# Another order of the projection pairs in a hybrid decoder block, and another place for the first SSD step

## The chip, the core and the metric

The kernel runs on one core of a Trainium2 chip. The metric is the device time of one execution in microseconds (us). Five engines work side by side, each through its own queue in order: TensorE (PE in the profile, its weight loads PEld), VectorE (DVE), ScalarE (ACT), GpSimd (POOL) and SyncE (SP). Loads and stores are DMAs, issued here from the queues of SP and ACT.

## The reference

One decoder layer over 1024 positions with a width of 1024, all in float32:

```
u    = rmsnorm(x)
proj = u @ w_in        # gate_a | gate_s | B_a | C_a | v_a | z | xBC | dt
y_a  = (B_a * causal_conv3(C_a * v_a)) @ w_a_out
xbc  = silu(causal_conv4(xBC) + b)                  # 16 tiles of x, 4 of B, 4 of C
y    = ssd_scan(x, softplus(dt), B, C) + d_skip * x # 32 heads, 4 groups, chunks of 128
y_s  = group_rmsnorm(y * silu(z)) @ w_s_out
h    = x + (sigmoid(gate_a) * y_a + sigmoid(gate_s) * y_s) @ w_o
v    = rmsnorm(h)
out  = rmsnorm(h + (silu(causal_conv3(v @ w_1) + b) * (v @ w_3)) @ w_down)
```

The SSD scan works on chunks of 128 positions, one group of 8 heads after the other: within a chunk a masked product of C, B and x, and between chunks a state of 128 x 512 that decays.

## The kernel before

**Products.** Precision comes from splitting each float32 operand in a high part (written by ACT, line 148) and a low part (the difference, on POOL or DVE, line 149), and adding three matmuls per pair of operands. A product of a 128-column weight block is 12 matmuls (line 259). The projection is made in *pairs* of two 128-channel blocks over all 1024 positions by a Strassen-Winograd scheme with 7 products instead of 8, so a pair is 84 matmuls. The seven results go through PSUM and are combined on DVE (lines 287 to 318) to the two output rows of 128 x 1024. The seven left operands (U) are made once and fill all 14 big buffers until the last pair has used them.

**Kinds of pairs.** 37 pairs are run by the two lists of the change, by kind and first block:
- `xb` (xBC): two s4 tiles for the inputs of the convolution; then for each channel block a convolution of one ACT and three DVE instructions over 128 x 1024 (lines 535 and 539), Silu (line 546) and a store to the DRAM buffer ssd_in (line 548). xb 0 to 14 are x of groups 0 to 3 (four blocks a group), xb 16 and 18 are B of groups 0, 1 and 2, 3; xb 20 and 22 are C of the same.
- `z`: two b4 tiles, Silu, store to ssd_in (lines 563 and 564).
- `ca`, `ba`: C_a, v_a and B_a of the short convolution; ca uses one s4 and one b4 tile, ba two s4 tiles. Four DVE instructions and a product; the result is stored.
- `gs`, `ga`: gates, two b4 tiles, Tanh and a store.

There are three s4 and three b4 tiles, so a pair's tiles are waited for if earlier ones are still in the convolution or in a store.

**The SSD beside the pairs.** `BEFORE` is run first. Then each product of a pair in `BESIDE` advances a clock by one tick, and the parts of the SSD's steps are called at fixed ticks: step s (group s // 8, chunk s % 8) has its base at D0 + DSTEP * s, and its eight parts at the offsets of STAGES: the loads m (line 633) and in (line 636, six blocks of ssd_in: four of x, one of B, one of C) at -9; the decay matrix on ACT at -6; transposes px, pb and the product pc (lines 648 to 652) with their consumers at -4; loads for z and the decay at -3; the matmuls pd, po and pst (lines 690 to 703) with DVE's adds and the state on POOL at 0; squares at 3; the norm's sum pn at 6, and after each fourth chunk a transpose pr. A step's loads and its store go through ACT's queue.

**Order.** These calls give each instruction a priority in program order. A planner that simulates the engines then fixes each queue's order: a later instruction goes ahead when its inputs and its buffers are free in the simulation. At run time each engine works through its queue in order.

**After the pairs** come y_a (64 products over half the positions at a time, two halves), s_out, out_proj and the feed-forward part. w_sums, eleven calls beside s_out and y_a, prepares sums and differences of w_down for the last products: two loads of 512 KB into s4 tiles (tile wd, line 793), four subtractions on DVE and POOL (line 784), four stores (line 801).

Of the kernel before, what the change touches and what calls it, by code (L numbers as in the profile page):

```python
# [39 lines left out]


BEFORE = (
    ("xb", 16), ("z", 0), ("xb", 18), ("z", 2), ("xb", 20), ("xb", 22), ("xb", 0), ("xb", 2),
)
BESIDE = (
# [4 lines left out]
)  # L50


D0, DSTEP = 11, 6
STAGES = LOAD_M, LOAD_IN, DECAY, TRANS, LOAD_Z, DIAG, SQUARES, NORM = -9, -9, -6, -4, -3, 0, 3, 6


# [1181 lines left out]
```

## Time and profile before

| what | value |
|---|---|
| median of 3 runs | 2004.32 us (2004.31 to 2005.55) |
| profiled execution | 2004.03 us, span 2002.3 us |
| granted TensorE clock, mean | 0.986 |
| PE busy | 96% of the span |
| DVE, POOL, ACT busy | 72%, 65%, 46% |

Lines of the timeline give start, length, engine, source line and operation with output <- inputs; where the engine stood idle just ahead, its idle time and what ended it follow in brackets. Sums over stretches give for each stretch the busy time of the engines and the number of their instructions, then the granted clock of TensorE, the DMA engines' busy share and what they moved. A table of waits names who waited, for whom, the total, the number of times and the longest. A tile's table gives minimum, median and maximum in ns, and the first and last start. Matmuls overlap in the pipeline, so their busy times can sum to more than a stretch.

The pairs of the two lists run from about 110 to 996 us; the SSD's matmuls from 289 to 996 us.

### The profile page before, as it was taken

How to read it: one execution, taken by the hardware profiler on the slowest of the kernel's cores; microseconds unless marked ns; L12 is line 12 of the kernel's file. 1: busy time of each engine (PE TensorE's matmuls, PEld its weight loads, DVE VectorE, ACT ScalarE, POOL GpSimd, SP SyncE). 2: the span in 40 equal slices, each digit the busy share in tenths (PEclk: the TensorE clock that was granted, in tenths of full speed). 3: DMA queues.
4: the chain of work that ended last, by engine and by line, in shares of the span. 5: the costliest groups of instructions: out<-in, count | busy, mean ns of one | idle time of the engine just before them, and what ended most of it. 6: DMA issues, size and time to landing. Idle time of an engine off the chain costs nothing.

```text
span 2002.3 us, 26005 instructions
## 1 busy us (share of the span) xinstructions
PE 1923.3 (96%) x8986; PEld 1575.2 (79%) x8986; DVE 1450.9 (72%) x1616; ACT 918.0 (46%) x1697; POOL 1292.9 (65%) x931
## 2 busy tenths in 40 slices
PE   6899989999999999998999999988999999999998
PEld 5778877788788778776788888877888888887886
DVE  8956886787888778786884724379877788884445
ACT  5354445556655855444443323354433333343434
POOL 7667776776767677677545423368887888853542
PEclk9999999999999999999999999998999999999999
DMA  4244234444534554387897645442322244477654
GB/s 153 51 141 143 95 121 153 148 152 144 190 119 151 167 168 144 113 267 254 317 409 251 225 151 188 159 165 81 130 85 102 104 153 153 153 242 261 217 184 157
DMA packets 180179, 338.46 MB, mean 169 GB/s; under 512 B 15280, under 2 KB 87760, under 8 KB 179024
## 3 DMA queue, kind: packets, MB, share of 16 engines
q1 hardware_dynamic: 93264, 253.95, 37.1%
q10 hardware_dynamic: 86784, 82.85, 13.0%
q8 instruction: 71, 1.16, 0.2%
q14 instruction: 60, 0.49, 0.1%
HBM read 247.34 MB, written 89.41 MB: 168 GB/s over the span
## 4 chain that ended last, share of the span: by engine, by line
PE 64%; DVE 14%; DMA 7%; issue 5%; POOL 4%; ACT 4%; ACTq 0%; SPq 0%; POOLq 0%; DVEq 0%
PE so L259 9%; PE ya L259 4%; DVE cv L539 4%; PE pt2up L259 3%; PE pt3up L259 3%; PE pb22up L259 3%; PE pt4up L259 3%; PE pb11up L259 3%; PE pt1up L259 3%; PE pb21up L259 3%; PE d L1031 2%; PE d L1032 2%; PE d L1033 2%; DMA wd<-in_w_down 1%; PE wo L904 1%
## 5 line engine op out<-in xcount | busy, mean ns | idle before, releaser
L539 DVE SCALAR_TENSOR_TENSOR cv<-xbc,scw,cv 128x1024 f32<-128x1024 f32 x72 | 128.8, 1800 | 20.8 <-ACT cv L535 20.5
L642 ACT ACTIVATE m<-m,tk 128x128 f32<-128x128 f32 x256 | 79.1, 391 | 101.0 <-DMA m<-acd 88.5
L539 DVE SCALAR_TENSOR_TENSOR fcv<-fci,fcw,fcv 128x1024 f32<-128x1024 f32 x44 | 85.9, 1953 | 28.5 <-ACT fcv L535 28.5
L149 POOL TENSOR_TENSOR l_ws<-raw_ws,h_ws 128x512 fp32r<-128x512 f32 x32 | 46.4, 1450 | 74.6 <-PE so L259 43.1
L148 ACT CAST h_ws<-raw_ws 128x512 fp32r<-128x512 f32 x64 | 39.4, 622 | 99.1 <-PE so L259 67.5
L259 PE MATMUL so<-yh,h_ws 128*128 128x512 f32 x256 | 68.8, 391 | 0.0
L259 PE MATMUL so<-yl,h_ws 128*128 128x512 f32 x256 | 68.6, 389 | 0.0
L259 PE MATMUL so<-yh,l_ws 128*128 128x512 f32 x256 | 68.5, 389 | 0.0
L149 POOL TENSOR_TENSOR l_wo<-raw_wo,h_wo 128x512 fp32r<-128x512 f32 x24 | 31.6, 1316 | 53.9 <-PE wo L905 36.5
L149 DVE TENSOR_TENSOR l_wo<-raw_wo,h_wo 128x512 fp32r<-128x512 f32 x24 | 25.2, 1050 | 51.7 <-ACT h_wo L148 26.9
L661 ACT ACTIVATE xe<-px,tk 128x64 f32<-128x64 f32 x256 | 55.5, 326 | 13.2 <-DVE xd L654 13.2
L148 ACT CAST h_wo<-raw_wo 128x512 fp32r<-128x512 f32 x48 | 29.6, 621 | 65.5 <-PE wo L905 32.7
L149 DVE TENSOR_TENSOR l_ws<-raw_ws,h_ws 128x512 fp32r<-128x512 f32 x32 | 26.0, 816 | 41.6 <-PE so L259 27.7
L259 PEld LDWEIGHTS so<-yl,h_ws 128*128 128x128 f32 x256 | 48.1, 188 | 10.0
L259 PEld LDWEIGHTS so<-yh,l_ws 128*128 128x128 f32 x256 | 48.1, 188 | 10.0
L259 PEld LDWEIGHTS so<-yh,h_ws 128*128 128x128 f32 x256 | 47.8, 188 | 9.7
L672 DVE TENSOR_TENSOR m<-m,cb 128x1024 f32<-128x1024 f32 x32 | 52.6, 1644 | 0.4
L149 POOL TENSOR_TENSOR l_wa<-raw_wa,h_wa 128x512 fp32r<-128x512 f32 x16 | 27.3, 1704 | 37.7 <-ACT h_wa L148 18.5
L903 PE MATMUL wo<-h_wo,mh 128*128 128x512 f32 x128 | 49.9, 391 | 1.2 <-ACT h_wo L148 1.2
L546 ACT ACTIVATE cv<-cv 128x1024 f32<-128x1024 f32 x24 | 25.5, 1062 | 55.1 <-DVE cv L539 55.1
L904 PE MATMUL wo<-l_wo,mh 128*128 128x512 f32 x128 | 50.0, 391 | 0.0
L905 PE MATMUL wo<-h_wo,ml 128*128 128x512 f32 x128 | 49.7, 391 | 0.0
(1063 smaller groups left out, 6710.4 us busy)
## 6 DMA issues: line engine op xcount, KB each, us to landing
m<-acd ACTq DMA_DIRECT2D x32, 512.0 KB, 5.5
raw_ws<-in_w_s_out SPq DMA_DIRECT2D x32, 512.0 KB, 4.2
ssd_in<-cv ACTq DMA_DIRECT2D x24, 512.0 KB, 2.6
in<-ssd_in ACTq DMA_DIRECT2D x32, 384.0 KB, 4.1
raw_wo<-in_w_o SPq DMA_DIRECT2D x24, 512.0 KB, 3.4
wd<-in_w_down SPq DMA_DIRECT2D x22, 512.0 KB, 6.1
td<-wd SPq DMA_DIRECT2D x44, 256.0 KB, 4.3
raw_1up<-in_w_up SPq DMA_DIRECT2D x22, 512.0 KB, 3.2
```

The source lines that it names most:

```text
L148: act.copy(hi, v)
L149: (eng or pool).tensor_tensor(lo, v, f32(hi), op=ALU.subtract)
L259: pe.matmul(ps, wt[:, k, :], ct[:, k, :], start=(start and n == 0), stop=(stop and n == 11),)
L539: dve.scalar_tensor_tensor(cv, ci[:, j : j + SEQ], w[:, j : j + 1], cv, op0=ALU.mult, op1=ALU.add)
L642: act.activation(m[:, h, :], m[:, h, :], AF.Relu, bias=a)
L661: act.activation(xe[:, hc], px[:, hc], AF.Copy, scale=tk[:, 2, cc, q, g * HG + h : g * HG + h + 1],)
L672: dve.tensor_tensor(m, m, cb.unsqueeze(1).to_broadcast([P, HG, P]), op=ALU.mult)
L903: pe.matmul(pss[t], mh, wh, start=k == 0, stop=False)
L904: pe.matmul(pss[t], mh, wl, start=False, stop=False)
L905: pe.matmul(pss[t], ml, wh, start=False, stop=k == NK - 1)
L1031: pe.matmul(ps, aa[0][:, ts], bb[0], start=k == 0, stop=False)
L1032: pe.matmul(ps, aa[0][:, ts], bb[1], start=False, stop=False)
```

## The change

The lists are put in another order and cut at another place, and D0 goes from 11 to 17:

```diff
 BEFORE = (
-    ("xb", 16), ("z", 0), ("xb", 18), ("z", 2), ("xb", 20), ("xb", 22), ("xb", 0), ("xb", 2),
+    ("xb", 16), ("z", 0), ("xb", 20), ("xb", 0), ("z", 2), ("xb", 2),
 )
 BESIDE = (
-    ("xb", 4), ("z", 4), ("xb", 6), ("z", 6), ("ca", 0), ("ca", 1), ("ba", 0),
-    ("xb", 8), ("z", 8), ("xb", 10), ("z", 10), ("ca", 2), ("ca", 3), ("ba", 2),
-    ("xb", 12), ("z", 12), ("xb", 14), ("z", 14), ("ca", 4), ("ca", 5), ("ba", 4),
-    ("ca", 6), ("ca", 7), ("ba", 6), ("gs", 0), ("gs", 2), ("gs", 4), ("gs", 6), ("ga", 6),
+    ("xb", 4), ("z", 4), ("xb", 6), ("z", 6), ("xb", 18), ("gs", 0), ("xb", 22), ("z", 8),
+    ("xb", 8), ("z", 10), ("xb", 10), ("gs", 2), ("ca", 0), ("ca", 1), ("ba", 0), ("z", 12),
+    ("xb", 12), ("z", 14), ("xb", 14), ("gs", 4), ("ca", 2), ("ca", 3), ("ba", 2),
+    ("ca", 4), ("ca", 5), ("ba", 4), ("ca", 6), ("ca", 7), ("ba", 6), ("gs", 6), ("ga", 6),
 )
-D0, DSTEP = 11, 6
+D0, DSTEP = 17, 6
```

BEFORE goes from 8 to 6 pairs, BESIDE from 29 to 31, that is from 203 to 217 ticks. The last part of the last SSD step is called at tick 203 before and 209 after. Nothing else in the source changes; the planner makes its order anew.

## The prediction

> **What bounds the kernel now.** I read the page first, then TensorE's waits, then sums over stretches, and last the timelines of two places.
>
> ```profile
> span 2002.3 us, 26005 instructions
> PE 1923.3 (96%) x8986; PEld 1575.2 (79%) x8986; DVE 1450.9 (72%) x1616; ACT 918.0 (46%) x1697; POOL 1292.9 (65%) x931
> 129.96 2.72 PE pb11z L259 x12
> 110.00:263.08 153.08, 153.08 (x672) 126.60 (x670) 0.99 0.35 118
> ```
>
> TensorE (PE) is the bound. A product of twelve matmuls takes 2.72 us (a row of the chain), a pair of seven 19.04 us. The last row is the sum of line 259 (all products) over 110 to 263 us, the pairs ahead of the SSD: PE has no hole there. So the front can lose but not gain, and what can be gained lies beside the SSD. The next two fences cut that part into four stretches: the first two pairs (xb4, z4); sixteen pairs up to z14; six pairs ca4 to ba6; five gate pairs. First line 259 alone, then line 690, whose 16 matmuls mark one SSD step.
>
> ```profile
> 263.08:309.70 46.62, 38.28 (x157) 30.20 (x156) 0.93 0.36 124
> 309.70:692.83 383.13, 326.16 (x1320) 243.54 (x1321) 0.99 0.49 154
> 692.83:842.10 149.27, 123.80 (x505) 93.70 (x504) 0.98 0.45 142
> 842.10:996.18 154.08, 122.19 (x483) 91.29 (x482) 0.97 0.82 270
> ...
> 263.08:309.70 46.62, 1.09 (x16) 0.85 (x16) 0.93 0.36 124
> 309.70:692.83 383.13, 20.58 (x288) 16.07 (x288) 0.99 0.49 154
> 692.83:842.10 149.27, 8.54 (x112) 6.69 (x112) 0.98 0.45 142
> 842.10:996.18 154.08, 6.57 (x96) 5.12 (x96) 0.97 0.82 270
> ```
>
> The columns are stretch, length, PE busy and matmuls, weight loads, granted clock, DMA share, GB/s. The busy column counts overlaps, so I use lengths: from each I take its matmuls of line 259 at 2.72/12 = 0.2267 us, and what remains is the price of the SSD steps in it, holes included.
> - A, 263 to 310: 46.62 - 157 x 0.2267 = 11.0 us for 1 step.
> - B, 310 to 693: 383.13 - 299.2 = 83.9 us for 18 steps, 4.66 each.
> - C, 693 to 842: 149.27 - 114.5 = 34.8 us for 7 steps, 4.97 each.
> - D, 842 to 996: 154.08 - 109.5 = 44.6 us for 6 steps, 7.43 each.
>
> Together 174.3 us for 32 steps. At B's price they would cost 149.1; the surplus sits in A (6.3) and D (44.6 - 6 x 4.66 = 16.6), and 2.2 in C.
>
> **A, the first step.** Timelines of PE, then of ACT:
>
> ```profile
> 262.17 1.07 PE L259 MATMUL pb22xb<-us4h,l_b22xb 128*128 128x512 f32 x4
> 288.91 1.09 PE L648 MATMUL px<-ident,in 128*128 128x128 f32 x4 [5.50 <-DMA in<-ssd_in]
> 291.72 1.91 PE L259 MATMUL pb11z<-ua11h,l_b11z 128*128 128x512 f32 x4
> 296.25 1.07 PE L259 MATMUL pt1z<-us1h,h_t1z 128*128 128x512 f32 x4
> ...
> 281.55 1.06 ACT L546 ACTIVATE cv<-cv 128x1024 f32<-128x1024 f32 x1 [3.66 <-DVE cv L539]
> 282.64 0.33 ACTq L548 DMA_DIRECT2D ssd_in<-cv  x1
> 285.34 0.97 ACTq L636 DMA_DIRECT2D in<-ssd_in  x2
> ```
>
> xb2, the last input of the first step, leaves PE at 263.1. Its second convolution leaves VectorE and ACT at 282.6, is written to DRAM, read back, and the transposes px start at 288.91: 25.8 us after the pair. They are placed at tick D0 - 4 = 7, 7 x 2.72 = 19.0 us after the pair. PE stands 5.50 us, and then runs at half speed for a while (1.91 us for four matmuls, 1.07 later).
>
> **D, the gates.** PE's waits and VectorE's waits in D, the instructions of the tile wd, and a step's po with and without a hole ahead of it:
>
> ```profile
> PE po L697 <- DVE gt L316: 4.4, 2, 3.2
> PE pb22g L259 <- DVE gt L316: 3.8, 1, 3.8
> ...
> DVE wd L784 <- DMA wd<-in_w_down: 18.8, 6, 4.9
> DVE wd L784 <- POOL wd L784: 6.5, 5, 2.7
> ...
> L793 SPq DMA_DIRECT2D wd<-in_w_down x22: 328/352/1350, 855.0 to 1064.9; - x22
> L784 DVE TENSOR_TENSOR wd<-wd x11: 679/1218/1785, 862.1 to 1069.2; 128x512 f32<-128x512 f32 x11
> ...
> 949.31 2.07 PE L697 MATMUL po<-in,st 128*128 128x128 f32 x8 [3.21 <-DVE gt L316]
> 925.31 1.16 PE L697 MATMUL po<-in,st 128*128 128x128 f32 x8
> ```
>
> PE waits for VectorE's adds into the gates (line 316), and VectorE had stood 25.3 us for w_sums, which prepares the down projection. Its two s4 tiles come free when ba6, the last pair that uses s4, is done (first load 855.0); from then its subtractions sit in VectorE's queue among SSD and gate work, waiting for 512 KB loads. That is D's surplus: 16.6 us for six waits, 2.8 each.
>
> **The change, part by part.**
>
> Work is neither added nor removed: 37 pairs (8 + 29 before, 6 + 31 after), 32 steps, the same DMAs. Order is all.
>
> 1. D0 from 11 to 17. xb2 again ends at tick 0, px goes to tick 13, 35.4 us after it, against 25.8 needed: 9.6 us of slack. Each step issues on ACT's queue its loads m, in, eb, zt and the store yd, on POOL the skip product, the state decay and the power; they keep their distance among themselves, and in is issued at tick 8 (21.8 us) where its data are written at about 22.3 (285.34 - 263.08), so ACT's queue is held half a microsecond at most, where four products' splits are ready ahead. A's surplus goes: -6.3. Late next: nothing that A shows; m and zt wait in B already.
>
> 2. Six pairs in BEFORE instead of eight. The stretch 110 to 263 has no hole with five xBC pairs in a row; alternation asks less of VectorE. 0, bounds 0 to +3 (a hole like A's half).
>
> 3. xb18 and xb22 (two pairs) move beside the SSD, gs0, gs2 and gs4 come forward. Two xBC pairs bring 12 convolution taps beside the SSD:
>
> ```profile
> L539 DVE SCALAR_TENSOR_TENSOR cv<-xbc,scw,cv 128x1024 f32<-128x1024 f32 x72 | 128.8, 1800 | 20.8 <-ACT cv L535 20.5
> L643 ACT ACT_TABLE_LOAD x12 | 15.4, 1283 | 0.2
> L546 ACT ACT_TABLE_LOAD x9 | 11.5, 1283 | 0.2
> 309.70:692.83 383.13, 375.03 (x1939) 303.25 (x1938) 302.11 (x377) 235.35 (x531) 275.53 (x207) 0.99 0.49 154
> 692.83:842.10 149.27, 144.28 (x742) 116.49 (x741) 122.78 (x146) 77.36 (x192) 106.20 (x77) 0.98 0.45 142
> ```
>
> 12 x 1.80 = 21.6 us of VectorE in some 730 us. It is busy 302.11 of 383.13 us in B (79%; columns PE, PEld, DVE, ACT, POOL) and 82% in C. The cover is that spare fifth; without it all 21.6 would show. I take +2, a tenth, as B hides nearly all of its taps. Function switches: 21 table loads in the two rows for twelve Silu pairs beside the SSD, so two more pairs add about 4, 5.1 us of ACT, which is busy 61% in B: 0, bound +5.
>
> 4. The tail. The SSD's last diagonal step is at tick 17 + 6 x 31 = 203 of 217, the end of ba6. D's six steps thus run beside ca and ba pairs, at C's price, and w_sums, still tied to ba6, meets only gs6 and ga6, without SSD. About ten steps run in the chain ca2 to ba6 (63 ticks / 6 = 10.5), where seven did in C. D's surplus goes: -16.6. C's small surplus grows: 10.5 x 0.31 = 3.3 instead of 2.2, +1.1. In gs6 and ga6 (some 40 us) two w_sums, at one per 20.7 us ((1069.2 - 862.1)/10), may still hold VectorE: 0 to 2 x 2.8 = 5.6. I take +3, the middle: the cause is there, but the SSD's adds that were queued behind it are not. What slips past the gates, some nine w_sums, runs beside y_a and s_out, where PE's only wait up to 1300 us and the waits of VectorE up to 1080 are
>
> ```profile
> PE pr L743 <- POOL yr L739: 0.4, 1, 0.4
> ...
> DVE wd L784 <- DMA wd<-in_w_down: 2.8, 1, 2.8
> DVE wd L784 <- DMA raw_ws<-in_w_s_out: 3.0, 1, 3.0
> 1000.00:1050.00 50.00, 50.00 (x222) 41.42 (x221) 40.63 (x41) 21.95 (x32) 20.96 (x13) 1.00 1.03 411
> ```
>
> so four w_sums cost PE nothing there, at 411 GB/s: 0 for the slipped ones; their bound is the third rival. On SP's queue loads and stores of w_sums follow the weights of gs6 and ga6, which have three raw tiles.
>
> Sum: -6.3 + 0 + 2 - 16.6 + 1.1 + 3 = -16.8 us. The profiled execution took 2004.03 us (span 2002.3 plus 1.7), close to the median 2004.32; 2004.0 - 16.8 = 1987.
>
> [...] In A the hole costs its 5.50 us and a slow start. [...]
>
> **The rivals.**
> - The first step waits still: something else on ACT (in order, 61% busy) delays in or m by more than the 9.6 us of slack. For it: ACT waits for the loads of m more than for anything (the row below). Against: B's steps have the same queue at 4.66. Then -16.8 + 6.3 = -10.5: 1994.
>
> ```profile
> L642 ACT ACTIVATE m<-m,tk 128x128 f32<-128x128 f32 x256 | 79.1, 391 | 101.0 <-DMA m<-acd 88.5
> ```
>
> - All at B's price, w_sums harmless: -25.2, without a loss elsewhere 1979; with B's cleanest steps perhaps 1974.
> - w_sums takes its harm along: D's 16.6 us come back in gs6, ga6, y_a and s_out. For it: DMA is at its fullest there. Against: the four that cost nothing. -6.3 + 2 + 1.1 = -3.2: 2001, no change that can be told (nine at 2.8 would be 25.2, and 2009).
> - Slower: the chain of nine ca and ba pairs (before: runs of three and six) lets VectorE fall ever further behind beside the SSD. For it: C is dearer than B, with VectorE busier (82 against 79%), and PE waits on it. At D's price of 7.43 instead of 4.97 the 10.5 steps cost +25.8: +9, 2013. It decides from 4.97 + 16.8/10.5 = 6.6 us per step on. Against: D's price came with w_sums in the queue, which isn't there until ba6 is done.
>
> **How the numbers follow.** The forecast 0.52 (own range 1980 to 1997), the first step still late 0.10 (1994), all clean 0.10 (1974 to 1979), w_sums 0.14 (2001), the long chain 0.14 (2013). A measurement tells about 0.2%, 4 us, from no change. Faster holds the first three cases, 0.72; same 0.14; slower 0.14. The range 1974 to 2006 leaves out the chain's case and little else.
>
> **What would show it.** Step 1: no PE wait px <- DMA in near the SSD's start, and first px about 35 us after xb2's last product. Step 3: VectorE near 80% beside the SSD and line 259's remainder at 4.4 to 4.9 us per step. Step 4: pd ends two pairs ahead of the mixer's end; wd's first load lies after ba6, near the end of the mixer; the waits on gt are gone or short. PE's busy time stays at 1923 us less the slow matmuls, and the mixer ends near 980. I am wrong if PE waits on VectorE in the ca and ba chain, or in y_a for weights.

## The result, and the profile after

The changed kernel takes 1977.03 us (median of 4 executions, 1975.95 to 1979.87) where before takes 2004.32 (1996.69 to 2005.55 in its 4); the ratio is 0.9874, with a 95% interval of 0.9847 to 0.9901. Beside the experiments below it was run again: 0.9862 (0.9848 to 0.9875). Forecast were 1987 us and a range of 1974 to 2006; the narrower range of its main case, 1980 to 1997, was missed by 3 us. The profiled execution took 1977.71 us; its page begins

```profile
span 1975.9 us, 25975 instructions
PE 1912.1 (97%) x8986; PEld 1567.8 (79%) x8986; DVE 1443.1 (73%) x1616; ACT 925.8 (47%) x1703; POOL 1303.6 (66%) x931
```

The counts of PE, DVE and POOL are those of before, so only order changed; ACT has six instructions more (its table loads went from 26 to 32). PE's busy time fell by 11 us, the span by 26.4. Stretches of the changed kernel, in the columns of the prediction: the first two pairs beside the SSD; xb6 to gs2; ca0 to gs4; the chain ca2 to ba6; gs6 and most of ga6. First the products (line 259), then pd (line 690):

```profile
225.83:261.66 35.83, 35.53 (x157) 29.11 (x156) 1.00 0.35 124
261.66:499.71 238.05, 199.59 (x816) 150.88 (x817) 1.00 0.50 159
499.71:697.84 198.13, 166.63 (x686) 126.52 (x684) 0.98 0.50 157
697.84:920.89 223.05, 191.94 (x782) 143.74 (x780) 1.00 0.46 142
920.89:960.00 39.11, 35.66 (x155) 28.59 (x155) 1.00 0.85 293
...
261.66:499.71 238.05, 12.04 (x176) 9.38 (x176) 1.00 0.50 159
499.71:697.84 198.13, 10.56 (x144) 8.12 (x144) 0.98 0.50 157
697.84:920.89 223.05, 12.04 (x176) 9.38 (x176) 1.00 0.46 142
920.89:960.00 39.11, 1.09 (x16) 0.85 (x16) 1.00 0.85 293
```

By the same subtraction the rests are 0.2 us without a step, 53.1 for 11 (4.82 each), 42.6 for 9 (4.74), 45.8 for 11 (4.16) and 4.0 for 1. Together 145.7 us where before had 174.3: 28.6 less. Some 2 us of it are lost elsewhere in the span. Each of these prices comes from one traced execution: in a second one of the changed kernel (r_after) the three long stretches have 56.7, 39.8 and 46.4 us, so single stretches move by some 3 us, and the chain's price holds (4.22 a step).

The first step, on PE and on ACT's queue:

```profile
224.92 1.07 PE L259 MATMUL pb22xb<-us4h,l_b22xb 128*128 128x512 f32 x4
261.20 0.60 PE L648 MATMUL px<-ident,in 128*128 128x128 f32 x4
...
241.46 0.34 ACTq L548 DMA_DIRECT2D ssd_in<-cv  x1
244.16 0.38 ACTq L636 DMA_DIRECT2D in<-ssd_in  x1
```

px stands 35.4 us after xb2's last product (225.83), with no idle time ahead of it. The end of the mixer: PE's waits from the chain ca2 to ba6 on; VectorE's for w_sums in gs6 and ga6; w_sums' first and last load:

```profile
PE pst L703 <- DVE yss L735: 1.9, 2, 1.3
PE pr L743 <- POOL yr L739: 1.6, 1, 1.6
PE po L697 <- DVE gt L318: 0.6, 1, 0.6
...
DVE wd L784 <- DMA wd<-in_w_down: 5.7, 2, 4.1
DVE wd L784 <- POOL wd L784: 2.5, 1, 2.5
...
L793 SPq DMA_DIRECT2D wd<-in_w_down x22: 332/382/841, 922.1 to 1135.0; - x22
```

VectorE still waits for w_sums, 8.2 us instead of 25.3, but of PE's waits for VectorE's adds into gates (`DVE gt`) 0.6 us are left, where the two rows shown of before had 8.2. The last pd lies at 921, y_a begins at 963.39.

### The profile page after: what moved, and what is told of

It reads as the page before. It is cut to its first block, busy times and chain, and to the rows that moved or that the text cites. A ratio compares the mean times of both kernels' runs of the same rounds, so it can differ in the third digit from the quotient of the medians.

```text
span 1975.9 us, 25975 instructions
## 1 busy us (share of the span) xinstructions
PE 1912.1 (97%) x8986; PEld 1567.8 (79%) x8986; DVE 1443.1 (73%) x1616; ACT 925.8 (47%) x1703; POOL 1303.6 (66%) x931
## 3 DMA queue, kind: packets, MB, share of 16 engines
q8 instruction: 71, 1.16, 0.2%
## 5 line engine op out<-in xcount | busy, mean ns | idle before, releaser
L539 DVE SCALAR_TENSOR_TENSOR cv<-xbc,scw,cv 128x1024 f32<-128x1024 f32 x72 | 132.1, 1847 | 17.1 <-ACT cv L535 16.8
L539 DVE SCALAR_TENSOR_TENSOR fcv<-fci,fcw,fcv 128x1024 f32<-128x1024 f32 x44 | 85.9, 1951 | 28.6 <-ACT fcv L535 28.5
L149 POOL TENSOR_TENSOR l_wo<-raw_wo,h_wo 128x512 fp32r<-128x512 f32 x24 | 32.5, 1354 | 35.1 <-PE wo L905 23.0
L665 POOL TENSOR_TENSOR in<-in,dsk 128x512 f32<-128x512 f32 x32 | 46.5, 1453 | 8.6 <-PE px L648 8.5
```

The lines of the kernel that those rows point to most:

```text
L149: (eng or pool).tensor_tensor(lo, v, f32(hi), op=ALU.subtract)
L539: dve.scalar_tensor_tensor(cv, ci[:, j : j + SEQ], w[:, j : j + 1], cv, op0=ALU.mult, op1=ALU.add)
L665: pool.tensor_tensor(xt, xt, dsk[:, 4 * g : 4 * g + 4].unsqueeze(2).to_broadcast([P, 4, P]), op=ALU.mult,)
```

## The experiments

Each time is a median beside runs of before on the same chip; before's median was 1999.15 us beside e1 to e4, 2004.14 beside r_after and e5 to e7, and 2004.15 beside e8 to e11, so the ratios are what is to be compared. "Less" in us is worked out from the ratio. Single executions spread: the 23 of before beside e1 to e4 lie between 1990.96 and 2005.93 us, and the trace of before that the prices come from took 2004.03. A difference of stretches is therefore a place to look at, and the ratio says what it is worth. The theory: the change does two things, it starts the first step when its inputs are there, and it keeps w_sums away from the SSD steps.

**e1: D0 alone**, on the lists of before.

```diff
-D0, DSTEP = 11, 6
+D0, DSTEP = 17, 6
```

> The lists of before with D0 = 17 alone, so that every SSD part comes six ticks later. Theory: the first step's wait for its inputs goes (6.3 us in stretch A of the prediction), the gates' stretch keeps its loss, as the last SSD steps and w_sums still meet there: 2004 - 6 = 1998 us. Rival, the hole only moves (something else in the first step is late): 2004. Rival, the offset is nearly all of the gain: under 1985.

1991.42 us, 0.9956 (0.9940 to 0.9972): 8.8 us less, 5.6 to 12 by the interval, which holds the 6.3. The first two pairs cost their products alone, and PE has no wait of px (line 259, the first two pairs and the gates):

```profile
261.91:297.73 35.82, 35.52 (x157) 29.12 (x156) 1.00 0.37 135
825.37:996.00 170.63, 137.08 (x540) 102.60 (x541) 0.97 0.88 292
```

The gates keep their loss: 170.63 - 540 x 0.2267 = 48.2 us. One thing is not in the theory: the sixteen pairs between cost 75.9 us for 18 steps instead of 83.9 (375.07 us with 1320 matmuls), and in e5, with D0 = 17 too, 77.9. The traced execution of e1 is one of its fastest (1984.83 us), so whether the offset has a worth there stays open.

**e2: the lists alone**, with D0 back at 11.

> The lists of the changed kernel with D0 = 11. Theory: px stands at tick 7, 19.0 us after xb2's last product, with data that need about 25.8, so the hole of 5 to 6 us and its slow start come back; all else as in the changed kernel: 1977 + 6 = 1983 us. Rival, alternation alone makes the inputs early enough: 1977, and no wait of px. Rival, the offset is the gain: above 1995.

1981.43 us, 0.9917 (0.9892 to 0.9942). The total is near the theory, its reason is not: px stands earlier than with D0 = 17 and yet waits almost nothing.

```profile
247.12 0.63 PE L648 MATMUL px<-ident,in 128*128 128x128 f32 x4 [0.60 <-DMA in<-ssd_in]
```

xb2 ended at 226.19, so the inputs took 20.9 us where the order of before took 25.8. The convolutions come through VectorE sooner: xb2's first tap starts 0.5 us ahead of the end of its products, and 4.6 us behind it in before. That z2 between xb0 and xb2 is the reason is read off the order and not tested apart. The rival on the hole was right. What D0 = 17 adds to the new lists is therefore not this wait (see e9 and e10).

**e3: before, with w_sums held back.** Two s4 tiles are taken after ba6 and read after the last gate (`gates` collects the gates' tiles).

```diff
+    gates = []
...
         for i, gt in enumerate(gts):
+            gates.append(gt)
...
     for item in BESIDE:
         run(*item)
+        if item == ("ba", 6):
+            hold = [s4(f"hold{i}") for i in range(2)]
+            for h in hold:
+                pool.memset(h[:, :1], 0.0)
+    for h in hold:
+        act.copy(h[:, :1], gates[-1][:, :1])
```

> Before, with two s4 tiles held from ba6 to the last gate, so that w_sums can't start among the gates; nothing is left out. Theory: VectorE's 25 us of waits for w_sums' loads leave the gates' stretch, whose surplus of 16.6 us goes, and the eleven w_sums cost nothing beside y_a and s_out: about 2004 - 15 = 1989 us. Rival, five gate pairs in a row are the cause (three b4 tiles, stores ahead of their reuse): 2004. Rival, w_sums takes its harm along: PE waits in y_a, 2000 or more.

1981.51 us, 0.9920 (0.9898 to 0.9942): 16 us less. Pairs and steps stand as before, so stretches C and D can be laid beside those of before (products, then pd, which has another line number here):

```profile
692.84:838.40 145.56, 122.82 (x505) 93.03 (x504) 1.00 0.45 146
838.40:980.00 141.60, 126.27 (x524) 96.88 (x523) 1.00 0.65 220
...
692.84:838.40 145.56, 7.66 (x112) 5.97 (x112) 1.00 0.45 146
838.40:980.00 141.60, 6.57 (x96) 5.12 (x96) 1.00 0.65 220
```

D's six steps cost 141.60 - 524 x 0.2267 = 22.8 us, 3.80 each instead of 7.43; among the gates PE waits for nothing that the profile lists. C costs 4.44 a step. The five gate pairs in a row are innocent, and w_sums, all of it beside y_a and s_out now, does little harm there: PE waits 2.1 us in all from 985 to 1300 us.

**e4: the transpose pr two ticks later**, on before; it asks why C cost 4.97 a step.

```diff
         pool.tensor_tensor(r[:, c % 4 : c % 4 + 1], rs, nhalf, op=ALU.pow)
+        yield
         if c % 4 == 3:
...
-        for o in STAGES:
+        for o in STAGES + (NORM + 2,):
```

> Before, with the transpose pr of each fourth chunk called two ticks after the power on POOL that it reads, instead of in the same tick. Theory on the chain of ca and ba pairs, whose steps I priced at 4.97 us and which cost 4.16 after: the difference is pr's wait for POOL (four waits, 6.5 us, two of them followed by a half-speed start), not load on VectorE. Then those waits go: 2004 - 6 to - 10, some 1996 us, and the stretch of ca4 to ba6 costs about 4.2 per step. Rival, VectorE's load is the price: pr's wait gives way to another, 2002 to 2005.

1999.84 us, 1.0009 (0.9993 to 1.0025): no change. In the stretch of the same six pairs (products, pd) the theory holds, 142.27 - 505 x 0.2267 = 27.8 us for 7 steps, 3.97 each. But other waits came (PE's, 226 to 940 us):

```profile
699.71:841.98 142.27, 123.62 (x505) 93.04 (x505) 1.00 0.48 148
...
699.71:841.98 142.27, 7.66 (x114) 5.97 (x112) 1.00 0.48 148
...
PE pc L652 <- DVE st L713: 3.5, 2, 3.1
PE pc L652 <- DVE gt L316: 3.1, 2, 1.6
PE pd L690 <- DVE m L672: 3.1, 3, 1.9
```

The hole, with the slow start behind it (last section), was what made C dear. Taking it away won nothing in the whole: the planner made another order with other holes, and PE's listed waits from 226 to 940 us come to 26.9 us where before has 26.7. My expectation of the total failed.

**e5: D0 = 17 and the hold, in the old order of the lists** (e1's and e3's edits together).

> The lists of before, with D0 = 17 and with the two s4 tiles held to the last gate. Theory: the change does two things and no more, it starts the first step with its inputs there and keeps w_sums away from the SSD; both together without the new order give 0.9956 x 0.992 = 0.988 of before, 1974 to 1976 us, the changed kernel's time within 0.3%. Rival, the new order has a worth of its own (alternation, the earlier start of the SSD): then this stays above the changed kernel by 6 us or more.

1975.21 us, 0.9854 (0.9839 to 0.9869); the changed kernel beside it had 0.9862.

> The changed kernel once more, beside the next three on one chip: about 0.987 of before, 1974 us where before has a median of 1999.

The two edits give all that the change gives, without its order. A worth of alternation or of the SSD's earlier start in the span does not show.

**e6: the changed kernel with the hold.**

> The changed kernel with two s4 tiles held from ba6 to the last gate. Theory: w_sums in gs6 and ga6, without SSD steps, costs nearly nothing (I had put 3 us there), so holding it brings 0 to 2 us: as the changed kernel. Rival, it still costs 2.8 us each there: 4 to 6 us faster. Rival, eleven w_sums beside y_a and s_out are one too many: slower.

1977.97 us, 0.9877 (0.9859 to 0.9894), overlapping 0.9862: the two w_sums in gs6 and ga6 cost nothing that can be told.

**e7: the changed kernel with gs0, gs2 and gs4 behind ba6 again.**

```diff
-    ("xb", 4), ("z", 4), ("xb", 6), ("z", 6), ("xb", 18), ("gs", 0), ("xb", 22), ("z", 8),
-    ("xb", 8), ("z", 10), ("xb", 10), ("gs", 2), ("ca", 0), ("ca", 1), ("ba", 0), ("z", 12),
-    ("xb", 12), ("z", 14), ("xb", 14), ("gs", 4), ("ca", 2), ("ca", 3), ("ba", 2),
-    ("ca", 4), ("ca", 5), ("ba", 4), ("ca", 6), ("ca", 7), ("ba", 6), ("gs", 6), ("ga", 6),
+    ("xb", 4), ("z", 4), ("xb", 6), ("z", 6), ("xb", 18), ("xb", 22), ("z", 8),
+    ("xb", 8), ("z", 10), ("xb", 10), ("ca", 0), ("ca", 1), ("ba", 0), ("z", 12),
+    ("xb", 12), ("z", 14), ("xb", 14), ("ca", 2), ("ca", 3), ("ba", 2),
+    ("ca", 4), ("ca", 5), ("ba", 4), ("ca", 6), ("ca", 7), ("ba", 6),
+    ("gs", 0), ("gs", 2), ("gs", 4), ("gs", 6), ("ga", 6),
```

> The changed kernel with gs0, gs2 and gs4 put back behind ba6, so that w_sums starts five pairs ahead of the end and about 3.5 SSD steps run among the gates. Theory: each step that meets w_sums costs 3.6 us more ((44.6 - 22.8) / 6, before against e3), so + 13: about 1987 us where the changed kernel has 1974. Rival, the gain lies in the earlier start and the first step: as the changed kernel.

1997.05 us, 0.9969 (0.9958 to 0.9980): 21 us more than the changed kernel, where I had 13. The gates' stretch (products, pd) and VectorE's waits in it:

```profile
846.66:996.00 149.34, 126.25 (x507) 97.33 (x506) 0.95 0.81 275
...
846.66:996.00 149.34, 4.38 (x64) 3.41 (x64) 0.95 0.81 275
...
DVE wd L785 <- DMA wd<-in_w_down: 24.0, 7, 7.4
DVE wd L785 <- POOL wd L785: 8.1, 3, 3.6
```

34.4 us for 4 steps, 8.6 each, and 32 us of waiting on VectorE: the harm came back with w_sums, at 4.4 us a step over the chain's 4.16 instead of the 3.6 that I took from before.

**e8: before, without VectorE's two subtractions in w_sums.** Part of what w_sums stores is then left uncomputed, so this is a measurement and no kernel to use.

```diff
-        sub(b11, b12, b11)
         sub(b12, b22, b12, pool)
-        sub(b22, b22, b11)
```

> Before, without the two subtractions on VectorE in each w_sums; its loads, its two subtractions on POOL and its stores stay, so part of what it stores is left uncomputed. Theory: what costs in the gates' stretch is VectorE's queue standing still for the loads of w_down, so this comes near e3: about 0.992 of before, - 16 us. Rival, the DMA traffic or POOL's share of w_sums among the gates is the cause: 0.998 or more of before.

1992.77 us, 0.9942 (0.9925 to 0.9959): 11.6 of e3's 16 us. In the gates VectorE waits for w_down no more, POOL does, and PE waits for POOL (the products of the gates' stretch; waits of POOL, then of PE, 837 to 985 us):

```profile
837.60:985.00 147.40, 123.79 (x507) 93.53 (x506) 0.98 0.89 306
...
POOL wd L784 <- DMA wd<-in_w_down: 14.8, 6, 5.5
...
PE pr L743 <- POOL yr L739: 3.7, 2, 3.4
```

The stretch's six steps cost 147.40 - 507 x 0.2267 = 32.5 us, 5.41 each: between before's 7.43 and e3's 3.80. So VectorE's share of w_sums carries the larger part of the harm. What is left may be POOL's or the DMA traffic's, which is still among the gates here (a share of 0.89); of POOL only the wait of 3.7 us is seen. Nor does e8 part waiting from work: it takes from VectorE the 25.3 us of waits, and also 20.2 us of subtractions that before has in D.

**e9: the changed kernel with D0 = 14. e10: with D0 = 11 again, on the same chip. e11: e5 with D0 = 14.**

> The changed kernel with D0 = 14. px then stands at tick 10, 27.2 us after xb2's last product; in e2 the inputs were there 20.9 us after it. Theory, the offset matters only until the inputs are there: no wait of px, time as the changed kernel, 0.986 to 0.987 of before. Rival, the offset has a worth beyond that: half way to e2, 0.989.

> The lists of the changed kernel with D0 = 11 once more, beside D0 = 14 on one chip. e2 had 0.9917 of before with a wait of px of only 0.6 us, so the first step's wait doesn't explain its distance to 0.987. If that distance is real, it shows again: 0.990 to 0.992. If it came from that chip's before, it goes: 0.987 to 0.988.

> e5 (lists of before, the two tiles held) with D0 = 14 instead of 17. px stands at tick 10, 27.2 us after xb2, with inputs that need 25.8 in this order: no wait of px, and half of the six parts that ran on behind the last gate end with it. Theory: as e5, 0.985, or up to 3 us faster. Rival, the slack of 1.4 us is too small in some runs: 0.987.

e9: 1998.45 us, 0.9969 (0.9957 to 0.9982). e10: 1985.28 us, 0.9906 (0.9886 to 0.9926). e11: 1979.99 us, 0.9886 (0.9867 to 0.9904); px waits for nothing there either, and yet it is 6 us behind e5, not level with it as expected. No theory of mine gave e9: px waits for nothing, and more than three quarters of the gain is gone. e10 shows e2's distance to the changed kernel again, some 9 us, so that is likely real, and no wait of px explains it (0.7 us in e10's trace). Part of it lies behind the pairs: from 960 to 1300 us PE waits 3.9 us in e2 and 5.8 in e10, 0.4 in the changed kernel. For e9 the traces show where. ACT's waits for the loads of m, and PE's longest waits, from 260 to 720 us, of the changed kernel and then of e9; last, ACT's waits for m in e10:

```profile
ACT m L642 <- DMA m<-acd: 43.4, 17, 5.3
...
PE pn L733 <- DVE ss L730: 3.9, 3, 1.8
PE pst L703 <- DVE yss L735: 3.5, 3, 1.9
...
ACT m L642 <- DMA m<-acd: 71.8, 21, 6.2
...
PE pr L743 <- POOL yr L739: 5.0, 2, 3.6
PE pt4g L259 <- ACT bk L669: 3.3, 1, 3.3
PE pb11z L259 <- ACT m1xb L285: 2.8, 1, 2.8
...
ACT m L642 <- DMA m<-acd: 56.9, 17, 5.9
```

In e9 ACT's queue stands 28 us longer behind m, and PE waits for ACT, 10.8 us in this stretch, which it hardly does in the changed kernel (0.3). e10 lies between in all three: 56.9 us behind m, 3.7 us of PE's waits for ACT, and the time. That goes together; no run changes m's place alone, so it isn't shown as the cause. Why this offset makes the planner place m so, and whether 17 is more than a lucky value, stays open: in the new lists 11, 14 and 17 give 0.9906, 0.9969 and 0.9862 to 0.9874, which is no trend. In the old lists with the hold they give 0.9920 (e3), 0.9886 (e11) and 0.9854 (e5), a steady fall. No kernel run here is clearly faster than the changed one; e5 equals it.

## Why the prediction was right, point by point

- **The first step, -6.3.** The number came: stretch A fell from 11.0 us with one step to 0.2 with none, and e1 shows the same with D0 alone. One step of the argument failed: I took 25.8 us for the inputs in the new order too; e2 shows 20.9. In e2 the new lists all but removed the hole without the offset (40.16 us with 157 matmuls and one step, 4.6 us of rest), so the two edits cover the same hole, and the credit that I gave to D0 belongs as much to the lists. What D0 = 17 adds to the new lists, some 9 us, was in no term of mine.
- **The front, 0.** Right: the 19.04 us per pair up to 226 us stayed (six pairs, 114.23 us).
- **xb18 and xb22 beside the SSD, +2.** Not contradicted, and not shown: the twenty steps from 262 to 698 us cost 95.7 us, 2.5 over B's price; r_after has 96.5 and e6, with the same lists, 92.6, so +2 can't be told from 0.
- **The tail.** The mechanism was right (e3 and e7), two sizes were off. The chain ca2 to ba6 was priced with C's 4.97 us a step; it cost 4.16, 8.9 us less over its 11 steps. C's price held a hole of 3.3 us in which pr waits for POOL, and a start at half speed behind it (pd took 1.97 us). e3's C has the order of before and the same hole, 3.5 us, but comes back at full speed (pd took 1.09 us): 4.44. e4, without that wait, has 3.97. And the +3 for w_sums in gs6 and ga6 measured nothing (e6). Those two terms are the distance between -16.8 and the -28.6 of the stretches. The two ratios say 25 and 28 us for the whole.
- **The rivals.** The late first step did not come. The long chain of ca and ba pairs did not slow down, it is the cheapest of the three long stretches. w_sums did not take its harm along: in e3 and e6 all of it runs beside y_a and s_out, where PE's waits come to 2.1 us in each. "All clean" (1974 to 1979 us) is what came, and had a chance of 0.10; it was too low because I counted a hole in C, and its slow start, as a price of the work.
- **What I did not see:** how much the planner's new order alone can move. e4, e9 and e11 are small edits of time slots that cost or failed to win 6 to 22 us.

## What to carry to other kernels

Where each engine works through its queue in order, work that a planner moves ahead into free time is not free if it waits for a load: it makes its queue wait, and all that stands behind it. Here that work and its waits together cost 16 us (e3). Price stages by what is left after their sure work, but look whether a hole sits in the stage whose price is carried over, and in more than one traced execution, as the same hole can cost more in one than in the next (behind one of 1.8 us po took 2.08 us in one execution of the changed kernel, behind one of 1.7 us at the same place 1.16 in the other). Where an offset or an order is planned anew, try several neighbours before one is given a meaning.

## What the runs showed of the hardware

How long PE stands idle did not tell whether it comes back at half speed. In the changed kernel half speed came after a hole of 1.82 us (po took 2.08 us, at a granted clock of 0.59 from 659.6 to 663.4 us, and 1.16 in before, where the clock was 1.00 from 925 to 930 us); in e9 full speed came after a hole of 3.33 us (1.21 and 1.09 us for four matmuls, at a granted clock of 1.00 from 372.5 to 380 us; in the changed kernel four take 1.07 at 1.00). Timeline of the changed kernel, then of e9:

```profile
658.18 0.35 PE L733 MATMUL pn<-ones,ss 128*128 128x1 f32 x2 [1.82 <-DVE ss L730]
659.59 2.08 PE L697 MATMUL po<-in,st 128*128 128x128 f32 x8
...
372.57 1.21 PE L259 MATMUL pt4g<-ua22h,h_t4g 128*128 128x512 f32 x4 [3.33 <-ACT bk L669]
373.62 1.09 PE L259 MATMUL pt4g<-ua22l,h_t4g 128*128 128x512 f32 x4
```

Nor did the order of the instructions decide it. The second traced execution of the changed kernel (r_after) has the same hole at the same place, 1.70 us, and goes on at full speed (po took 1.16 us, at a granted clock of 1.00 from 501 to 696 us); and C's hole ahead of pr is followed by half speed in before (a granted clock of 0.68 from 814 to 822 us), but not in e3 (1.00), with the same matmuls around it. Timelines of r_after, of before and of e3:

```profile
657.50 0.35 PE L733 MATMUL pn<-ones,ss 128*128 128x1 f32 x2 [1.70 <-DVE ss L730]
658.81 1.16 PE L697 MATMUL po<-in,st 128*128 128x128 f32 x8
...
813.68 0.37 PE L743 MATMUL pr<-ident,yr 128*4 128x128 f32 x1 [3.34 <-POOL yr L739]
813.99 1.97 PE L690 MATMUL pd<-m,xd 128*64 128x128 f32 x16
...
812.52 0.27 PE L746 MATMUL pr<-ident,yr 128*4 128x128 f32 x1 [3.49 <-POOL yr L742]
812.72 1.09 PE L693 MATMUL pd<-m,xd 128*64 128x128 f32 x16
```

The slow start costs before some 2.5 us: from pr to the end of the same products (pt1cv) it takes 7.66 us, e3 5.12.

What decides between half and full speed after a hole was not shown.
